# Second FFN projection of a decoder block: sixteen of 22 k tiles by seven block products, with the weight sums formed in HBM

## The chip, the cores and the metric

The kernel runs on one core of a Trainium2 chip. The metric is the device time of one execution in microseconds; times of a kernel are given as the median of its runs. All matrices are float32; TensorE takes them as fp32r.

## The reference

One decoder layer on 512 tokens of width 1024. What matters here is its second sub-layer, a SwiGLU FFN with 2816 hidden channels, and the final norm:

```python
h2 = rms_norm(x, norm2_g) * (1.0 + scale2) + shift2
f_g, f_u = jnp.split(h2 @ w_ffn_in, 2, axis=-1)          # (512, 1024) @ (1024, 5632)
x = x + gate2 * ((jax.nn.silu(f_g) * f_u) @ w_ffn_out)   # (512, 2816) @ (2816, 1024)
...
return rms_norm(x, final_norm_g)
```

Ahead of it stand the conditioning (adaLN), the combined input projection, a gated MLP mixer, a sparse attention and their projections.

## The kernel before

**Precision.** Every matrix operand is split into a rounded high part `hi` (ScalarE, a copy) and a rest `lo` (VectorE, raw minus hi). A product is three matmuls (`mm3`, L51 to L55: hi x hi, hi x lo, lo x hi). One matmul takes 128 rows of k, 128 columns of the stationary operand and up to 512 (here 256 or 512) columns of the moving one.

**Weight stream.** `add_w` enters a weight chunk of 1024 elements a partition into a list; `issue` starts its load into one of three `raw` buffers from SyncE's queue, `prep` makes `hi` and `lo` (three buffers each, L112 and L116), `ensure(upto)` does both in the list's order, and `get(i, ahead=2)` prepares two chunks beyond the one that is used.

**The order of work is written out by hand.** Each engine has one queue and runs it in the order in which the code emits. An instruction waits by semaphore for its operands and for the buffer that it overwrites; what stands behind it on its engine waits as well.

**First FFN projection.** For the steps `q` from -2 to 17 a block of 256 columns of `w_ffn_in` is multiplied as a 2 x 2 block product with seven products of blocks instead of eight (`sprod`, 256 moving columns; `s_issue` loads, `s_prep` splits the next step's weights and forms their sums). The products accumulate in PSUM tiles `R`; ScalarE copies seed one product's accumulator from another's (L1653, L1665). `gtile` holds the 22 channel tiles of silu(f_g) x f_u, `gq`. During these steps `last_mod` loads and accumulates the last section of the conditioning.

**Second FFN projection.** The 22 k tiles are in two classes. For eight (12 to 19, `KZ`) the product is again a 2 x 2 block product by seven: k halves of four tiles, token halves of 256, column halves of 512. `a_sum` forms the sums of A blocks (`gq`), `w_sub` the differences of weight blocks in SBUF, both on VectorE; `a_hi`, `a_lo`, `w_hi`, `w_lo` split; `zprod(k, ka, kw, start)` issues one product's 24 matmuls onto the accumulators `Z[k]` (PSUM tiles `pfo`, two banks each), `z_copy` seeds one accumulator from another, `z_out` and `z_add` bring one product's result to another accumulator through SBUF. The other 14 tiles (`KC`) are done directly afterwards: for both column halves `h`, chunk by chunk (two k tiles), `opt_a_mm` adds onto the same accumulators for each of four token tiles; `g_split` splits `gq`. For h = 1 the last token tile is computed in two pieces of 256 columns (`z` in the code), and the last three chunks go token tile by token tile.

**What follows a column half.** `resid` (L1162) takes a token tile of an accumulator, multiplies it by the gate (`rt`), adds the residual stream (`xr`; both VectorE) and squares it with a sum over the row (ScalarE, L1167). `scale_g` multiplies by the final gain (`xo`), `row_rstd` makes the norm's factor (GpSimd has a part), `finish` scales and stores. For h = 0 the four token tiles' `resid` and `scale_g` stand after all its chunks, beside the matmuls of h = 1.

```python
for n_, i in enumerate(ids[:-3] if h else ids):
    kts = stream[i]["kts"]
    if h == 0:
        g_split(2 * n_ + 2)
    hi, lo = get(i)
    ...
if h == 0:
    for tk in range(4):
        resid(pb[tk], 0, 512, 0, tk, gate_b[2])
        ...
        scale_g(0, 512, tk)
```

Of the kernel before, what the change touches and what calls it, by code (L numbers as in the profile page):

```python
# [9 lines left out]
F32 = mybir.dt.float32  # L10
# [18 lines left out]
def block_kernel(ctx: ExitStack, tc: tile.TileContext, x, positions, w_ada, b_ada, w_in,  # L29
# [239 lines left out]
    KZ, KC = (list(range(12, 16)), list(range(16, 20))), list(range(12)) + [20, 21]  # L269
    W_FO = [[add_w(w_ffn_out, KC[k:k + 2], 512 * h, 512) for k in range(0, len(KC), 2)] for h in range(2)]  # L270
# [1205 lines left out]
    GHOME = ["E1", None, "E3", None, "E0", None, ("S1_4", "S1_5"), ("S1_6", "S1_7"), "S2_2", "S2_3", "E7", None,  # L1476
             "S2_4", "S2_5"]
    spare = []

    def g_home(n):  # L1480
        h = GHOME[n]
        if h is None:
            return spare.pop()
        if isinstance(h, tuple):
            return [base.tile([128, S], F32R, name="gs", tag=t, bufs=1) for t in h]
        if h[0] == "S":
            t = base.tile([128, 2, S], F32R, name="gs", tag=h, bufs=1)
        else:
            t = ffn[0].tile([128, 4, S], F32R, name="gs", tag=h, bufs=1)
            spare.append((t[:, 2], t[:, 3]))  # L1490
        return t[:, 0], t[:, 1]
# [9 lines left out]
    zr, zw, za = {}, {}, {}  # L1501
    ZW = {"T1": ("E2", "E4"), "T2": ("E1", "E3"), "T3": ("E0", "E7"), "T4": ("E2", "E4"), "B22": ("E1", "E3")}
    ZA = {"A11": 0, "S1": 4, "S2": 6, "A12": 0, "S3": 4, "S4": 6, "A22": 0}

    def z_issue(name):
        kh, h = {"B11": (0, 0), "B12": (0, 1), "B21": (1, 0), "B22": (1, 1)}[name]
        for c in range(2):
            if name == "B11" or name == "B12" and c == 0:
                t = base.tile([128, 2, S], F32, name="raw", tag="raw", bufs=RAWB)
                ts = [t]  # L1510
            elif name == "B12":
                ts = [ffn[0].tile([128, 2, S], F32, name="zraw", tag="F0", bufs=1)]
            elif name == "B22":
                ts = [base.tile([128, 2, S], F32, name="zraw", tag=f"S2_{2 + c}", bufs=1)]
            else:
                ts = [base.tile([128, 1, S], F32, name="zraw", tag=f"S1_{4 + 2 * c + e}", bufs=1) for e in range(2)]
            k = KZ[kh][2 * c]
            for t in ts:
                n = t.shape[1]
                SY.dma_start(t, w_ffn_out[k * 128:(k + n) * 128, h * 512:h * 512 + 512].rearrange("(j p) n -> p j n", p=128))  # L1520
                k += n
            zr[name, c] = ts

    def z_parts(ts, *others):
        o = 0
        for t in ts:
            n = t.shape[1]
            yield (t,) + tuple(x_[:, o:o + n] for x_ in others)
            o += n

    def w_hi(key, c, src):
        if key in ZW:
            t = ffn[0].tile([128, 2, 2, S], F32R, name="zw", tag=ZW[key][c], bufs=1)
            zw[key, c] = (t[:, 0], t[:, 1])
        else:
            zw[key, c] = tuple(base.tile([128, 2, S], F32R, name=n, tag=n, bufs=3) for n in ("hi", "lo"))
        for t, hi in z_parts(zr[src, c], zw[key, c][0]):
            A.activation(hi, t, AF.Copy)

    def w_lo(key, c, src):  # L1540
        for t, hi, lo in z_parts(zr[src, c], *zw[key, c]):
            V.tensor_sub(lo, t, f(hi))

    def w_sub(o, a, b, c):

        (o_,), (b_,) = zr[o, c], zr[b, c]
        for a_, ob, bb in z_parts(zr[a, c], o_, b_):
            V.tensor_sub(ob, a_, bb)

    def a_block(name):  # L1550
        kh, th = {"A11": (0, 0), "A21": (0, 1), "A12": (1, 0), "A22": (1, 1)}[name]
        return gz[kh][:, :, th * 256:(th + 1) * 256]


    AT_ = {"A11": "A11", "A12": "A12", "A22": "A22", "S1": "A21", "S4": "A21", "S2": "A11", "S3": "A11"}

    def a_hi(key):
        za[key] = tuple(base.tile([128, 4, 256], F32R, name="za", tag=f"S2_{ZA[key] + e}", bufs=1) for e in range(2))
        A.activation(za[key][0], a_block(AT_[key]), AF.Copy)

    def a_lo(key):
        V.tensor_sub(za[key][1], a_block(AT_[key]), f(za[key][0]))

    def a_sum(key):
        a = {n: a_block(AT_[n]) for n in AT_}
        if key == "S1":
            V.tensor_add(a["S1"], a_block("A21"), a["A22"])
        elif key == "S2":
            V.tensor_sub(a["S2"], a["S1"], a["A11"])
        elif key == "S4":  # L1570
            V.tensor_sub(a["S4"], a["A12"], a["S2"])
        else:
            V.tensor_sub(a["S3"], a["A22"], a["S2"])

    def z_first():
        return [(lambda: w_hi("B11", 0, "B11"), lambda: w_lo("B11", 0, "B11")),
                (lambda: (a_hi("A11"), w_hi("B11", 1, "B11")), lambda: (a_lo("A11"), w_lo("B11", 1, "B11"))),
                (lambda: None, lambda: (w_sub("B11", "B12", "B11", 0), a_sum("S2"))),
                (lambda: (w_hi("T1", 0, "B11"), a_hi("S1")),
                 lambda: (w_sub("B11", "B12", "B11", 1), w_lo("T1", 0, "B11"), a_lo("S1")))]  # L1580
# [39 lines left out]
    for q in range(-2, NQ):  # L1620
# [8 lines left out]
        if q >= NQ - 2:  # L1629
            z_issue(("B11", "B12")[q - NQ + 2])  # L1630
# [27 lines left out]
        if q == NQ - 1:  # L1658
            z_issue("B21")
# [4 lines left out]
        sprod(R[1], S2_, TB[2], False)  # L1664
        A.activation(R[2], R[1], AF.Copy)  # L1665
# [22 lines left out]
        if q == 10:  # L1688
            for b_ in (3, 2):
                mbank[0] = b_  # L1690
                sec_tasks(one=True)
        if q == NQ - 2:
            a_sum("S1")
    z_issue("B22")
# [4 lines left out]
    def scale_g(c0, n, tk):  # L1699
        if not xo:  # L1700
            for k in range(2):
                t = ffn[0].tile([128, 2, D], F32, name="xo", tag=f"E{5 + k}", bufs=1)
                xo.extend((t[:, 0], t[:, 1]))
        cs_ = slice(c0, c0 + n)
        V.tensor_mul(xo[tk][:, cs_], xt[tk][:, cs_], fng[:, cs_])
# [10 lines left out]
    def zprod(k, ka, kw, start):  # L1716
        if start:
            Z[k] = [bank(ZB[k][e], "pfo") for e in range(2)]
        (ah, al) = za[ka]
        for c in range(2):  # L1720
            wh, wl = zw[kw, c]
            for e in range(2):
                o = slice(e * 128, (e + 1) * 128)
                for j in range(2):
                    mm3(Z[k][e], (ah[:, 2 * c + j, o], al[:, 2 * c + j, o]), (wh[:, j], wl[:, j]),
                        start and c + j == 0, c + j == 2, skip_group_check=True)

    def z_copy(dst, src):
        Z[dst] = [bank(ZB[dst][e], "pfo") for e in range(2)]
        for e in range(2):  # L1730
            A.activation(Z[dst][e], Z[src][e], AF.Copy)
# [7 lines left out]
    def z_add(dst, src):  # L1739
        for e in range(2):  # L1740
            V.tensor_add(Z[dst][e], Z[dst][e], Z["s", src][e])

    zprod(0, "A11", "B11", True)
    w_hi("T1", 1, "B11")
    a_hi("S2")
    w_lo("T1", 1, "B11")
    while left:
        left.pop(0)()
    w_sub("B11", "B22", "B11", 0)
    a_lo("S2")  # L1750
    z_copy(1, 0)
    zprod(3, "S1", "T1", True)
    w_sub("B11", "B22", "B11", 1)
    for c in range(2):
        w_hi("T2", c, "B11")
        w_lo("T2", c, "B11")
    a_hi("A12")
    w_hi("B21", 0, "B21")
    a_sum("S4")
    a_lo("A12")  # L1760
    a_sum("S3")
    z_out(3)
    zprod(1, "S2", "T2", False)
    w_hi("B21", 1, "B21")
    a_hi("S3")
    for c in range(2):
        w_lo("B21", c, "B21")
    for c in range(2):
        w_sub("B12", "B22", "B12", c)
    for c in range(2):  # L1770
        w_hi("T3", c, "B12")
    a_lo("S3")
    z_copy(2, 1)
    zprod(0, "A12", "B21", False)
    for c in range(2):
        w_lo("T3", c, "B12")
    a_hi("S4")
    for c in range(2):
        w_hi("B22", c, "B22")
    a_lo("S4")  # L1780
    for c in range(2):
        w_lo("B22", c, "B22")
    zprod(2, "S3", "T3", False)
    for c in range(2):
        w_sub("B11", "B21", "B11", c)
    a_hi("A22")
    for c in range(2):
        w_hi("T4", c, "B11")
    a_lo("A22")
    for c in range(2):  # L1790
        w_lo("T4", c, "B11")
    z_out(2)
    zprod(1, "S4", "B22", False)
    fng = ffn[0].tile([128, D], F32, name="fng", tag="F0", bufs=1)
    P.dma_start(fng, rows_bcast(final_norm_g, D))
    st["limit"] = 1 << 30
    ensure(W_FO[0][0])
    zprod(2, "A22", "T4", False)
    g_split(2)

    for h in range(2):
# [100 lines left out]
```

## Time and profile before

| | |
|---|---|
| median of 3 runs | 830.08 us (829.76 to 830.33) |
| the profiled execution | 829.8 us |
| span of its profile | 828.0 us |
| mean granted TensorE clock | 0.998 |
| PE, VectorE, ScalarE, GpSimd busy | 815.7, 672.2, 413.6, 108.5 us |
| moved by DMA | 109.10 MB, mean 132 GB/s |

The profile is one execution on the chip. PE is TensorE's matmuls, PEld its weight loads, DVE VectorE, ACT ScalarE, POOL GpSimd, SP SyncE (its queue of transfers is SPq). Times are us from the span's start, "mean ns" is of one instruction. In a timeline line stand the start, the duration, the engine, the line of the code, the operation, output and operands by the program's names, the shapes, the count, and in brackets the idle time of that engine before it with what ended it. In a windows line stand the stretch, its length, the busy time and instruction count of each engine, the granted clock, the DMA engines' busy share and GB/s. Matmuls are pipelined, so the step from one start to the next is what one costs.

### The profile page before, as it was taken

The page shows a single profiled execution, that of the slowest core. Times are in us where ns is not written, and L with a number is a line of the kernel's source. Part 1 is how long each engine was busy: PE and PEld are TensorE (multiplying, and loading weights), DVE is VectorE, ACT ScalarE, POOL GpSimd, SP SyncE. Part 2 cuts the span into 40 slices and gives each one's busy share as a digit, 9 for nine tenths or more (in the row PEclk, how much of TensorE's full clock was granted, in tenths as well). Part 3 has the DMA queues.
Part 4 walks back from the last instruction along what each step waited for, and adds up shares of the span by engine and source line. Part 5 has one row for each costly group of instructions (what it writes and reads, how often), then busy time and mean ns, then how long its engine had stood idle before and what let it go on. Part 6 is the DMA issues. An engine that isn't in the chain of part 4 may idle for free.

```text
span 828.0 us, 12858 instructions
## 1 busy us (share of the span) xinstructions
PE 815.7 (99%) x4980; PEld 730.0 (88%) x4980; DVE 672.2 (81%) x1161; ACT 413.6 (50%) x722; POOL 108.5 (13%) x101
## 2 busy tenths in 40 slices
PE   7999999999999999999999999999999999999996
PEld 6889889988888888988888899999999999888885
DVE  7989788798899558886697969799998888984635
ACT  5674544323322236665536586555555555563322
POOL 2060032362353411000000000000000000000001
PEclk9999999999999999999999999999999999999999
DMA  9974352423445562057631403445533335143212
GB/s 299 311 201 118 102 178 78 121 85 101 124 136 180 195 181 74 26 158 231 197 102 47 157 27 128 124 152 159 168 111 103 103 102 155 50 153 102 77 51 103
DMA packets 95677, 109.10 MB, mean 132 GB/s; under 512 B 5616, under 2 KB 76272, under 8 KB 95616
## 3 DMA queue, kind: packets, MB, share of 16 engines
q1 hardware_dynamic: 92512, 101.37, 40.2%
q0 software_dynamic: 2384, 6.10, 2.3%
q8 instruction: 39, 0.64, 0.3%
q10 hardware_dynamic: 720, 0.82, 0.3%
q14 instruction: 22, 0.18, 0.1%
HBM read 105.90 MB, written 2.10 MB: 130 GB/s over the span
## 4 chain that ended last, share of the span: by engine, by line
PE 96%; DMA 1%; DVE 1%; issue 0%; SPq 0%; ACT 0%; POOLq 0%; POOL 0%; DVEq 0%
PE pb L55 9%; PE pb L53 9%; PE pb L54 9%; PE R L53 8%; PE R L54 8%; PE R L55 8%; PE pfo L55 5%; PE pfo L53 5%; PE pfo L54 5%; PE pav L54 2%; PE pav L53 2%; PE pav L55 2%; PE pgb L53 2%; PE pgb L54 2%; PE pgb L55 2%; PE po L54 2%
## 5 line engine op out<-in xcount | busy, mean ns | idle before, releaser
L112 ACT ACTIVATE hi<-raw 128x1024 fp32r<-128x1024 f32 (+2 forms) x80 | 82.5, 1034 | 105.4 <-PE pb L54 39.9
L116 POOL TENSOR_TENSOR lo<-raw,hi 128x1024 fp32r<-128x1024 f32 x29 | 73.0, 2522 | 127.8 <-ACT hi L112 122.1
L116 DVE TENSOR_TENSOR lo<-raw,hi 128x1024 fp32r<-128x1024 f32 (+2 forms) x44 | 53.0, 1210 | 41.4 <-ACT hi L112 41.2
L53 PE MATMUL pb<-h,hi 128*128 128x512 f32 (+1 forms) x192 | 74.6, 388 | 0.0
L55 PE MATMUL pb<-h,lo 128*128 128x512 f32 (+1 forms) x192 | 73.9, 385 | 0.0
L54 PE MATMUL pb<-hl,hi 128*128 128x512 f32 (+1 forms) x192 | 73.9, 385 | 0.0
L177 DVE SCALAR_TENSOR_TENSOR acc<-mraw,cols,acc 128x512 f32<-128x512 f32 x49 | 40.1, 818 | 17.9 <-DMA mraw<-in_w_ada_dram 16.9
L55 PE MATMUL pfo<-hi,gs 128*128 128x512 f32 (+1 forms) x126 | 46.4, 369 | 0.0
L54 PE MATMUL pfo<-lo,gs 128*128 128x512 f32 (+1 forms) x126 | 46.4, 368 | 0.0
L53 PE MATMUL pfo<-hi,gs 128*128 128x512 f32 (+1 forms) x126 | 46.4, 368 | 0.0
L53 PE MATMUL R<-tb,sx 128*128 128x256 f32 x160 | 45.2, 282 | 0.0
L54 PE MATMUL R<-tb,sx 128*128 128x256 f32 x160 | 45.1, 282 | 0.0
L55 PE MATMUL R<-tb,sx 128*128 128x256 f32 x160 | 45.0, 281 | 0.0
L55 PE MATMUL R<-tb,lo 128*128 128x256 f32 x160 | 44.8, 280 | 0.0
L53 PE MATMUL R<-tb,hi 128*128 128x256 f32 x160 | 44.8, 280 | 0.0
L54 PE MATMUL R<-tb,hi 128*128 128x256 f32 x160 | 44.6, 279 | 0.0
L55 PEld LDWEIGHTS pb<-h,lo 128*128 128x128 f32 x192 | 36.0, 187 | 7.3
L54 PEld LDWEIGHTS pb<-hl,hi 128*128 128x128 f32 x192 | 36.0, 188 | 6.9
L53 PEld LDWEIGHTS pb<-h,hi 128*128 128x128 f32 x192 | 36.0, 188 | 6.9
L54 PE MATMUL pav<-lo,h 128*128 128x256 f32 x128 | 35.8, 279 | 0.0
L53 PE MATMUL pav<-hi,h 128*128 128x256 f32 x128 | 35.7, 279 | 0.0
L55 PE MATMUL pav<-hi,hl 128*128 128x256 f32 x128 | 35.7, 279 | 0.0
(392 smaller groups left out, 2655.4 us busy)
## 6 DMA issues: line engine op xcount, KB each, us to landing
raw<-in_w_ffn_in_dram SPq DMA_DIRECT2D x44, 512.0 KB, 4.6
raw<-in_w_in_dram SPq DMA_DIRECT2D x40, 512.0 KB, 3.9
mraw<-in_w_ada_dram SPq DMA_DIRECT2D x28, 512.0 KB, 4.1
raw<-in_w_ffn_out_dram SPq DMA_DIRECT2D x17, 512.0 KB, 3.8
s<-in_w_ada_dram SPq DMA_DIRECT2D x30, 256.0 KB, 5.6
raw<-in_w_proj_a_dram SPq DMA_DIRECT2D x8, 512.0 KB, 4.8
raw<-in_w_proj_b_dram SPq DMA_DIRECT2D x8, 512.0 KB, 4.6
raw<-in_w_in_dram SPq DMA_DIRECT2D x9, 256.0 KB, 4.7
```

The source lines that it names most:

```text
L53: T.matmul(o, wh, rh, start=start, stop=False, **kw)
L54: T.matmul(o, wh, rlo, start=False, stop=False, **kw)
L55: T.matmul(o, wlo, rh, start=False, stop=stop, **kw)
L112: A.activation(hi[:, :m], e["raw"][:, :m], AF.Copy)
L116: e["lo"].tensor_sub(lo[:, :m], e["raw"][:, :m], f(hi[:, :m]))
L177: V.scalar_tensor_tensor(o, w, cs[:, j:j + 1], o, op0=OP.mult, op1=OP.add)
```

## The change

Sixteen k tiles (4 to 19) instead of eight go by the seven products, with k halves of eight tiles; six (0 to 3, 20, 21) stay direct. A product now takes four weight chunks instead of two, 48 matmuls instead of 24. The four combinations of weight blocks that the products need are no longer formed on VectorE: GpSimd's queue issues 32 transfers of 512 KB from HBM to HBM, copies and adding transfers (`accum_op`), that build `wsum` 1 to 4; they are emitted during the steps of the first projection. All weight chunks, blocks and sums alike, now go through the common stream (`get`). A operands are in two halves (`c`), the first of which is four separate tiles of 512 columns. Signs are moved into the copies (`scale=-1.0`) and into `z_add`. The order at the end is changed: direct chunks of column half 0 come before the last product, S4 with block (1, 1), whose four chunks carry the residual steps of half 0 (`res0`); then `z_add`, then half 1's three chunks, token tile by token tile.

```diff
-    KZ, KC = (list(range(12, 16)), list(range(16, 20))), list(range(12)) + [20, 21]
-    W_FO = [[add_w(w_ffn_out, KC[k:k + 2], 512 * h, 512) for k in range(0, len(KC), 2)] for h in range(2)]
+    KZ, KC = (list(range(4, 8)) + list(range(12, 16)), list(range(8, 12)) + list(range(16, 20))), [0, 1, 2, 3, 20, 21]
+
+    dram = ctx.enter_context(tc.tile_pool(name="dram", bufs=1, space=bass.MemoryType.DRAM))
+    wsum = {n: dram.tile([1024, 512], F32, name=f"wsum{n}") for n in (1, 2, 3, 4)}
...
+    for key in ((0, 0), 1, 2, (1, 0), 3, 4):
+        add_z(key)
+    W_FO = [add_fo(0)]
+    add_z((1, 1))
+    W_FO.append(add_fo(1))
+
+    def wsum_steps():
+
+        def step(c, *moves):
+            o = slice(256 * c, 256 * c + 256)
+
+            def fn():
+                for n, add, src in moves:
+                    if isinstance(src, tuple):
+                        k = KZ[src[0]][2 * c] * 128
+                        src = w_ffn_out[k:k + 256, 512 * src[1]:512 * src[1] + 512]
+                    else:
+                        src = wsum[src][o]
+                    if add:
+                        P.dma_start(wsum[n][o], src, accum_op=OP.add)
+                    else:
+                        P.dma_start(wsum[n][o], src)
+            return fn
+
+        return [step(c, *m) for c in range(4) for m in (
+            ((1, 0, (0, 0)), (3, 0, (0, 1))), ((1, 1, (0, 1)), (3, 1, (1, 1))), ((2, 0, 1),), ((2, 1, (1, 1)),),
+            ((4, 0, 2),), ((4, 1, (1, 0)),))]
...
+    def z_first():
+        def b(k):
+            return lambda: ensure(wseq[wseq.index(W_Z[0, 0][0]) + k])
+        st["limit"] = 1 << 30
+        return [(b(0), lambda: a_hi("A11", 0), lambda: a_lo("A11", 0)),
+                (b(1), lambda: a_hi("A11", 1), lambda: a_lo("A11", 1)),
+                (lambda: None, lambda: a_sum("S2", 0)),
+                (b(2), lambda: a_sum("S2", 1))]
...
+    def zprod(k, ka, kw, start, tasks):
         if start:
             Z[k] = [bank(ZB[k][e], "pfo") for e in range(2)]
+        for c, i in enumerate(W_Z[kw]):
+            wh, wl = get(i)
+            for fn in tasks[c]:
+                fn()
+            ah, al = za[ka, c // 2]
             for e in range(2):
                 o = slice(e * 128, (e + 1) * 128)
                 for j in range(2):
+                    k_ = 2 * (c % 2) + j
+                    mm3(Z[k][e], (ah[:, k_, o], al[:, k_, o]), (wh[:, j], wl[:, j]),
+                        start and c + j == 0, c + j == 4, skip_group_check=True)
...
+    zprod(0, "A11", (0, 0), True, [[outs_left, hi_("S1", 0)], [lo_("S1", 0), hi_("S1", 1)], [lo_("S1", 1), hi_("S2", 0)],
+                                   [lo_("S2", 0), hi_("S2", 1)]])
+    z_copy(1, 0, -1.0)
+    zprod(3, "S1", 1, True, [[lo_("S2", 1)], [sm_("S4", 0), hi_("A12", 0)], [sm_("S4", 1), hi_("A12", 1)],
+                             [lo_("A12", 0)]])
     z_out(3)
+    zprod(1, "S2", 2, False, [[lo_("A12", 1)], [sm_("S3", 0)], [sm_("S3", 1), hi_("S3", 0)], [load_fng]])
+    z_copy(2, 1, -1.0)
+    zprod(0, "A12", (1, 0), False, [[lo_("S3", 0), hi_("S3", 1)], [lo_("S3", 1)], [hi_("A22", 0)],
+                                    [lo_("A22", 0), hi_("A22", 1)]])
+    zprod(2, "S3", 3, False, [[lo_("A22", 1)], [], [hi_("S4", 0)], [lo_("S4", 0), hi_("S4", 1)]])
     z_out(2)
+    zprod(2, "A22", 4, False, [[lo_("S4", 1)], [lambda: z_add(3, 2, V.tensor_sub)], [lambda: g_split(2)],
+                               [lambda: g_split(4)]])
+
+    for n_, i in enumerate(W_FO[0]):
+        hi, lo = get(i)
+        g_split(2 * n_ + 6)
         for tk in range(4):
+            opt_a_mm(Z[0][tk] if tk < 2 else Z[2][tk - 2], tk, hi, lo, stream[i]["kts"], gT, 22, False)
+    pb = [Z[0][0], Z[0][1], Z[2][0], Z[2][1]]
+
+    def res0(tk):
+        def fn():
+            resid(pb[tk], 0, 512, 0, tk, gate_b[2])
+            scale_g(0, 512, tk)
+        return fn
+
+    zprod(1, "S4", (1, 1), False, [[res0(tk)] for tk in range(4)])
+    z_add(1, 3, V.tensor_add)
+    last = bank(7, "pfo")
+    A.activation(last[:, :256], Z[3][1][:, 256:], AF.Copy)
+    pb = [Z[1][0], Z[1][1], Z[3][0], Z[3][1], last]
+    ids = W_FO[1]
+    ch = [get(i, 2 - k) for k, i in enumerate(ids)]
+    for tk in range(4):
...
```

In `zprod`, `get(i)` puts the split of the chunk after next on ScalarE's and VectorE's queues, then the `tasks` of this chunk follow, then the matmuls.

More of the change, by code (lines that the diff above doesn't have):

```diff
@@ L1483, in g_home @@
             return spare.pop()
[L1484 to L1490, printed above, removed]
+        t = ffn[0].tile([128, 4, S], F32R, name="gs", tag=h, bufs=1)
+        spare.append((t[:, 2], t[:, 3]))
         return t[:, 0], t[:, 1]
@@ L1498, in g_split @@
             gT[m] = (hi, lo)
[L1501 to L1522, printed above, removed]
@@ L1540, in w_lo @@
[L1540 to L1555, printed above, removed]
@@ L1557, in a_hi @@
[L1557 to L1573, printed above, removed]
@@ new lines, in block_kernel, with a_parts, z_sub, a_hi @@
+    AT_ = {"A11": (0, 0), "A21": (0, 1), "A12": (1, 0), "A22": (1, 1), "S1": (0, 1), "S4": (0, 1), "S2": (0, 0),
+           "S3": (0, 0)}
+    def a_parts(name, c):
+        kh, th = AT_[name]
+        o = slice(th * 256, (th + 1) * 256)
+        if c:
+            return [gz[kh][:, :, o]]
+        return [gq[4 + 4 * kh + e][:, o] for e in range(4)]
+    def z_sub(t, c):
+        return [t] if c else [t[:, e] for e in range(4)]
+    def a_hi(key, c):
+        h = ZA[key][c]
+        if isinstance(h, tuple):
+            t = tuple(base.tile([128, 4, 256], F32R, name="za", tag=n, bufs=1) for n in h)
+        else:
+            t = ffn[0].tile([128, 2, 4, 256], F32R, name="za", tag=h, bufs=1)
+            t = (t[:, 0], t[:, 1])
+        za[key, c] = t
+        for a, o in zip(a_parts(key, c), z_sub(t[0], c)):
+            A.activation(o, a, AF.Copy)
@@ L1628, in block_kernel @@
         ps = [ffn[0].tile([128, 256], F32, name="ps", tag="rt", bufs=2) for _ in range(2)]
-        if q >= NQ - 2:
-            z_issue(("B11", "B12")[q - NQ + 2])
+        if q == NQ - 2:
+            for i in W_Z[0, 0][:2]:
+                issue(i)
         t0, t1 = slice(0, 256), slice(256, 512)
@@ L1737, in z_out, with z_add @@
             A.activation(Z["s", src][e], Z[src][e], AF.Copy)
-    def z_add(dst, src):
+    def z_add(dst, src, op):
         for e in range(2):
[L1741 to L1756, printed above, removed]
```

194 lines of the change are left out of this document (71 added, 123 removed).

## The prediction

> **What bounds the kernel now.** I read the page's engine totals and slices first, then the chain that ended last.
>
> ```profile
> PE 815.7 (99%) x4980; PEld 730.0 (88%) x4980; DVE 672.2 (81%) x1161; ACT 413.6 (50%) x722; POOL 108.5 (13%) x101
> PE   7999999999999999999999999999999999999996
> DVE  7989788798899558886697969799998888984635
> PE 96%; DMA 1%; DVE 1%; issue 0%; SPq 0%; ACT 0%; POOLq 0%; POOL 0%; DVEq 0%
> ```
>
> TensorE is busy in nearly the whole span and carries 96% of the chain. So a matmul taken away counts in full, but only where nothing else then makes PE wait. The stretches that the change touches, in the windows view (PE, PEld, DVE, ACT, POOL busy us with instruction counts, granted clock, DMA share, GB/s):
>
> ```profile
> 490.00:700.00 210.00, 210.00 (x1769) 209.77 (x1769) 184.63 (x253) 123.47 (x221) 0.00 (x0) 1.00 0.42 127
> 700.00:720.00 20.00, 20.00 (x105) 16.90 (x104) 19.93 (x23) 12.62 (x17) 0.00 (x0) 1.00 0.21 71
> 720.00:740.00 20.00, 20.00 (x88) 16.14 (x87) 18.64 (x21) 12.97 (x17) 0.53 (x1) 1.00 0.32 103
> 740.00:760.00 20.00, 20.00 (x88) 16.18 (x87) 10.93 (x14) 6.56 (x10) 0.00 (x0) 1.00 0.42 135
> ```
>
> From 490 to 700 us run the first FFN projection's block products (256 columns), from 704 to 743 the seven products of the second projection (512 columns), then its direct k tiles. PE has no gap in any of them. VectorE is full in the products' 40 us (weight differences are formed there) and half idle afterwards.
>
> **Part 1: matmuls.** The tile view of the projection's accumulators, and PE's timeline over one direct chunk of 24 matmuls and the next:
>
> ```profile
> L53 PE MATMUL pfo<-hi,gs x126: 277/392/403, 743.0 to 820.6; 128*128 128x512 f32 x98, 128*128 128x256 f32 x28
> L53 PE MATMUL pfo<-zw,za x40: 389/394/400, 709.6 to 742.4; 128*128 128x512 f32 x40
> L53 PE MATMUL pfo<-hi,za x16: 392/396/400, 704.0 to 725.7; 128*128 128x512 f32 x16
> 770.78 0.39 PE L53 MATMUL pfo<-hi,gs 128*128 128x512 f32 x1
> 776.38 0.39 PE L53 MATMUL pfo<-hi,gs 128*128 128x512 f32 x1
> 781.83 0.39 PE L53 MATMUL pfo<-hi,gs 128*128 128x512 f32 x1
> ```
>
> L54 and L55 have the same counts: 3 x (98 + 40 + 16) = 462 matmuls of 512 columns and 84 of 256. A direct k tile costs 21 of 512 and 6 of 256, because the last token tile of the second column half is done in two pieces. Eight tiles fewer: 168 of 512 and 48 of 256 go. Seven products over eight k tiles instead of four add 7 x 4 x 2 x 3 = 168 of 512. What remains saved is 48 matmuls of 256 columns, at 210 us / 1769 = 0.119 us: **-5.7 us**. That is all the change can win; a matmul of 512 columns takes 0.227 to 0.233 us (5.45 and 5.60 us for 24), 0.23 below.
>
> **Part 2: the wait before the last direct tiles.** The new order ends with the three direct chunks of column half 0, then the product S4 (1,1) into the accumulators of half 1, then the addition of the saved product (`z_add`), then half 1's three chunks. Into the four chunks of that product the change puts the four residual steps of half 0. PE's next matmul accumulates onto what `z_add` writes, and `z_add` stands behind all four residuals in VectorE's queue. The same instructions, from the timeline of before:
>
> ```profile
> 776.58 1.06 ACT L112 ACTIVATE hi<-raw 128x1024 fp32r<-128x1024 f32 x1 [3.49 <-PE pfo L55]
> 777.67 1.22 DVE L116 TENSOR_TENSOR lo<-raw,hi 128x1024 fp32r<-128x1024 f32 x1 [3.17 <-ACT hi L112]
> 778.81 0.68 DVE L1165 TENSOR_TENSOR rt<-pfo,gate2b 128x512 f32<-128x512 f32 x1
> 779.53 0.69 DVE L1166 TENSOR_TENSOR xr<-xr,rt 128x512 f32<-128x512 f32 x1
> 780.26 0.63 ACT L1167 ACTIVATE rt<-xr 128x512 f32<-128x512 f32 x1 [2.62 <-DVE xr L1166]
> 780.87 0.68 DVE L1165 TENSOR_TENSOR rt<-pfo,gate2b 128x512 f32<-128x512 f32 x1
> 786.47 0.63 ACT L1167 ACTIVATE rt<-xr 128x512 f32<-128x512 f32 x1 [1.39 <-DVE xr L1166]
> 787.10 1.05 ACT L112 ACTIVATE hi<-raw 128x1024 fp32r<-128x1024 f32 x1
> ```
>
> In before the four residuals follow each other 2.06 us apart (778.81 to 780.87) under a long stretch of PE. In the changed order each is followed by the split of a further weight chunk: ScalarE can only make `hi` after the residual's Square, VectorE `lo` after `hi`, the next residual after `lo`. One round is rt to xr 0.72, to Square 0.73, to hi 0.63, to lo 1.09, to the next rt 1.14: 4.31 us, against 12 x 0.23 = 2.76 us that PE needs for a chunk. Counted from the product's first matmul (776.38 is such a moment, a chunk's first matmul): hi at 0.20, lo at 1.29, first rt at 2.43, fourth at 2.43 + 3 x 4.31 = 15.36, `z_add` at + 2.06 = 17.42, its first half done 0.69 later, at 18.1. PE ends the product at 48 x 0.23 = 11.0. **PE waits 7.1 us.** Everything behind it (three chunks, residuals, normalization) moves by that; the new tail is the old one.
>
> **Part 3: the clock after that wait.** The only long PE idle in this trace stand at its two ends:
>
> ```profile
> 4.86 9.30 PE L444 MATMUL warm<-cst 128*128 128x128 f32 x63 [4.86 <-DMA cst<-in_consts_dram]
> 6.00:8.00 2.00, 2.00 (x11) 2.00 (x10) 1.83 (x8) 1.14 (x1) 0.75 (x2) 1.00 1.02 399
> 8.00:10.00 2.00, 2.00 (x16) 2.00 (x15) 1.86 (x6) 1.20 (x4) 0.15 (x1) 1.00 1.02 394
> 10.00:12.00 2.00, 2.00 (x21) 2.00 (x20) 1.83 (x7) 1.80 (x3) 1.32 (x4) 1.00 1.15 323
> 820.83 0.28 PE L55 MATMUL pfo<-hi,gs 128*128 128x256 f32 x1
> 824.00:825.00 1.00, 0.00 (x0) 0.00 (x0) 0.09 (x1) 0.15 (x1) 0.00 (x0) 0.94 0.05 18
> 825.00:826.00 1.00, 0.00 (x0) 0.00 (x0) 0.00 (x0) 0.00 (x0) 0.00 (x0) 0.50 1.01 388
> ```
>
> PE's last matmul ends at 821.1; the granted clock is 0.94 in 824 to 825 and 0.50 after, so it fell at 824.9, 3.8 us into the idle. At the start the same matmul goes at 11 in 2 us, then 16, then 21: half pace until about 9.0, 4.2 us after PE began. A wait of 7.1 us is longer than 3.8, so PE comes back at half pace and loses half of some 4.2 us: **+2.1 us** (bounds 0, if the clock holds, and 3.5, if half pace lasts as long as the wait did). The Trainium skill, page "TensorE: Matmul & The Clock Gate", part 1 on the clock gate, has the clock halved after at least one idle window of about 3.4 us and full after a busy one; the trace's 3.8 and 4.2 agree. By its 3.4 us the loss would be an estimated 1.7 us.
>
> **Part 4: the start of the products.** In the last step of the first projection ScalarE now makes the first A operand in four pieces of 256 columns, ahead of the copy that seeds R[2]:
>
> ```profile
> 695.84 0.36 ACT L1653 ACTIVATE R<-R 128x256 f32<-128x256 f32 x1
> 696.14 0.36 ACT L1643 ACTIVATE fs<-R 128x256 f32<-128x256 f32 x1
> 697.32 1.05 ACT L1559 ACTIVATE za<-gq 128x1024 fp32r<-128x1024 f32 x1
> 699.21 0.38 ACT L1665 ACTIVATE R<-R 128x256 f32<-128x256 f32 x1
> 699.65 0.39 PE L53 MATMUL R<-tb,sx 128*128 128x256 f32 x1
> ```
>
> Before, the copy ends at 699.59 and PE needs it at 699.65. Four pieces at 0.30 put 1.2 us in; 0.54 us of idle ahead of 697.04 takes up part. **+0.6 us** (0 to 0.9).
>
> **Part 5: what is covered.** In the products VectorE loses eight weight differences and gains 14 more weight splits. Per product of 11.0 us it has four `lo`, one A operand to split and at most one A sum to form, each of these two as large as two `lo`: 8 x 1.14 = 9.1 us. A raw buffer is taken for 3.8 us of landing, 1.1 of hi and 1.1 of lo, 6.0 us; three of them must turn round in 8.3. Without that cover each late us is a us. The formation of sums, 32 moves of 512 KB, stands on GpSimd's queue:
>
> ```profile
> DMA  9974352423445562057631403445533335143212
> q1 hardware_dynamic: 92512, 101.37, 40.2%
> raw<-in_w_ffn_out_dram SPq DMA_DIRECT2D x17, 512.0 KB, 3.8
> 486.27 0.57 POOL L1404 DMA_DIRECT2D gate2b<-in_b_ada_dram  x1
> 727.62 0.53 POOL L1795 DMA_DIRECT2D fng<-in_final_norm_g_dram  x1 [240.78 <-DVE zw L1542]
> ```
>
> Nothing else is on that queue from 486 to 727, so the moves start about 487, each after the one it depends on; nobody waits behind them except the final gain's load, used 60 us later. Price: 101.37 MB took 0.402 x 828 = 333 us of all 16 engines, so 512 KB takes 1.72. No row shows a transfer that adds; its bounds are one load's price (32 moves, 55 us) and, with four times that for the 16 adds, 138 us. I take twice (reads two operands): 83 us. With 0.42 x 210 = 88 us of present use in the 210 us, 171 fit. Cost 0, with the rival below as its other end.
>
> **Sum.** -5.7 + 7.1 + 2.1 + 0.6 = +4.1 us. The profiled execution took 829.8 us (span 828.0 and 1.8 around it), 0.3 under the median: 833.9 for it, **834.2 us** for the median.
>
> **Rivals.** *The clock holds* (it falls later into an idle here, or the wait is under 3.8): +2.0, 832.1 us; the two ends of the trace speak against it. *The adds are dear*: at 3 times a load's price the engines are full (88 + 28 + 16 x 1.72 x 3 = 199), and loads and sums come late. At four times 226 us are wanted of 210, 16 us more: 850 us. For it: no row bounds an add, and the DMA slices show 0.4 to 0.5 from 520 to 600 against 0.3 in the 80 us after; against: sums are needed only from about 705, loads are issued a step ahead. *Faster*: the wait is 3r - 5.8 us for a round of r us; without Part 3 the change gains if r is under 3.5. If ScalarE and VectorE had the chunks' splits done ahead, r would be 2.06 and the wait 0.4: 830.1 - 5.7 + 0.6 + 0.4 = 825.4 us. Against: only three hi/lo buffers, and both queues run in the order written, in which the 2.62 and 1.39 us of ScalarE's waits on xr stand.
>
> **How the numbers follow.** Forecast 0.60, clock holds 0.17, dear adds 0.15, faster 0.06, and 0.02 for a wait so short that the terms cancel. A measurement of this kernel can tell about 0.2%, 1.7 us. Faster by more: 0.06. Within: 0.08 (0.02 and some third of the clock case, whose 2.0 us lies close). Slower: 0.86. Range: the clock case with Part 4 at 0 and the wait 0.5 shorter gives 831.0; above, Part 3's 3.5 and a first part of the dear adds give 840.0.
>
> **What would show it.** Right: one PE gap near 7 us ahead of the last 90 matmuls, put down to `z_add`; the granted clock at 0.5 after it; 498 matmuls on these accumulators; a gap under 1 us before the R[2] products. Wrong: no such gap, or gaps of PE between 490 and 700 with DMA share near 1, or waits for sums after 710.

## The result, and the profile after

| | before | after |
|---|---|---|
| median | 830.21 us (829.76 to 830.75) | 837.23 us (835.77 to 837.75) |
| ratio, 95% interval | | 1.0081 [1.0064, 1.0099] |
| the profiled execution, its span | 829.8, 828.0 us | 837.66, 835.9 us |
| mean granted clock | 0.998 | 0.992 |

The change makes the kernel 7.0 us slower; the forecast was 834.2 us in a range of 831.0 to 840.0. The page of after: engine totals, the slices of PE and VectorE, the chain that ended last.

```profile
PE 813.8 (97%) x4932; PEld 726.4 (87%) x4932; DVE 681.2 (81%) x1191; ACT 423.7 (51%) x746; POOL 131.2 (16%) x133
PE   7999999999999999999999999999999999999965
DVE  7989788798899558886797878899999888877465
PE 57%; DVE 14%; DMA 4%; ACT 2%; issue 1%; POOLq 0%; POOL 0%; ACTq 0%; DVEq 0%
```

PE is less busy than before, 813.8 us against 815.7, in a longer span; the last two slices of PE read 6 and 5, where before had 9 and 6. The chain now runs through VectorE, 14% against 1%. The waits view (engine, tile and line that waited, what it waited for: total us, times, longest) names both places, and the chain's pieces (start, us) show what the long one is made of:

```profile
PE pfo L53 <- DVE pfo L1758: 7.1, 1, 7.1
PE R L53 <- ACT R L1675: 0.4, 1, 0.4
```

```profile
794.20 0.96 ACT hi L112
795.18 1.22 DVE lo L116
796.41 0.61 DVE rt L1210
797.05 0.70 DVE xr L1211
797.90 0.47 issue
798.55 0.96 ACT hi L112
...
805.11 0.61 DVE rt L1210
805.75 0.70 DVE xr L1211
...
807.08 0.70 DVE pfo L1758
807.92 0.77 PE pfo L53
808.69 0.43 PE pfo L54
...
812.10 0.41 PE pfo L53
812.51 0.23 PE pfo L54
```

```profile
797.83 0.63 ACT L1212 ACTIVATE rt<-xr 128x512 f32<-128x512 f32 x1 [2.68 <-DVE xr L1211]
```

One round: `hi` on ScalarE, `lo` on VectorE, the residual's `rt` and `xr`, then 0.47 us that the chain calls issue and that the timeline, in the second fence, fills with the Square on ScalarE, then the next `hi`. 794.20 to 798.55 is 4.35 us. After the fourth comes `z_add` (L1758), and only then PE's first matmul of the last tiles, 7.1 us late. Those matmuls start 0.43 us apart until 812.5, 0.23 after. In the windows view the clock of that place, and the stretch of the first projection beside the moves:

```profile
490.00:700.00 210.00, 210.00 (x1769) 209.73 (x1768) 186.69 (x260) 124.03 (x225) 22.51 (x31) 1.00 0.75 205
805.00:810.00 5.00, 2.08 (x5) 1.72 (x6) 4.53 (x7) 1.97 (x4) 0.00 (x0) 0.55 0.00 0
810.00:815.00 5.00, 5.00 (x18) 3.92 (x18) 0.59 (x1) 0.00 (x0) 0.00 (x0) 0.76 0.00 0
```

The clock's deficit there, 0.45 and 0.24 of 5 us, is 3.45 us, so 6.9 us at half. In 490 to 700 the DMA share went from 0.42 to 0.75 with PE full. The tile view of the accumulators, and from the page GpSimd's transfers (packets, MB, share of 16 engines' span) and the issues (KB, us to landing):

```profile
L53 PE MATMUL pfo<-hi,za x112: 389/395/500, 705.9 to 800.0; 128*128 128x512 f32 x112
L53 PE MATMUL pfo<-hi,gs x54: 277/395/767, 772.8 to 826.5; 128*128 128x512 f32 x42, 128*128 128x256 f32 x12
```

```profile
q0 software_dynamic: 8144, 22.88, 11.4%
wsum<-in_w_ffn_out_dram POOLq DMA_DIRECT2D x24, 512.0 KB, 8.4
```

Before, q0 was

```profile
q0 software_dynamic: 2384, 6.10, 2.3%
```

11.4% of 835.9 less 2.3% of 828.0 us: the 32 moves took 76 us of all 16 engines, 2.4 each.

**Where 7.9 us of the profiled executions are** (829.8 to 837.66; first and last matmul of each stage in the two traces): the stages ahead of the change ended 1.2 us later, which no other kernel with this change repeated; the first projection took 0.7 us more, 0.4 of it the wait on R; the second took 120.8 us from first to last matmul against 116.8, so +4.0; from there to the end 1.9 more. The last 1.9 us are in no part of the prediction. The last store lands at 826.5 before and 832.4 after, and the span ends 1.5 and 3.5 us later. What stands there in the trace, though none of the views lists it, is GpSimd's closing instruction, DRAIN:

| kernel | transfers that GpSimd issues | DRAIN starts | lasts | span ends |
|---|---|---|---|---|
| before | 36 | 822.81 | 3.73 us | 828.0 |
| after | 68 | 828.73 | 6.34 us | 835.9 |

### The profile page after: what moved, and what is told of

The parts are those of the page before. It is cut to its first block, busy times and chain, and to the rows that moved or that the text cites. A ratio compares the mean times of both kernels' runs of the same rounds, so it can differ in the third digit from the quotient of the medians.

```text
span 835.9 us, 12907 instructions
## 1 busy us (share of the span) xinstructions
PE 813.8 (97%) x4932; PEld 726.4 (87%) x4932; DVE 681.2 (81%) x1191; ACT 423.7 (51%) x746; POOL 131.2 (16%) x133
## 3 DMA queue, kind: packets, MB, share of 16 engines
q0 software_dynamic: 8144, 22.88, 11.4%
## 4 chain that ended last, share of the span: by engine, by line
PE 57%; DVE 14%; DMA 4%; ACT 2%; issue 1%; POOLq 0%; POOL 0%; ACTq 0%; DVEq 0%
PE R L53 8%; PE R L54 8%; PE R L55 8%; DMA mraw<-in_w_ada_dram 4%; PE pfo L53 4%; PE pfo L55 4%; PE pfo L54 4%; DVE acc L177 3%; DVE sco L704 2%; DVE m L700 2%; PE pb L53 2%; PE pb L55 2%; PE pb L54 2%; PE po L54 2%; PE po L53 2%; PE po L55 2%
## 5 line engine op out<-in xcount | busy, mean ns | idle before, releaser
L112 ACT ACTIVATE hi<-raw 128x1024 fp32r<-128x1024 f32 (+2 forms) x100 | 103.8, 1039 | 101.3 <-PE pb L54 44.4
L116 DVE TENSOR_TENSOR lo<-raw,hi 128x1024 fp32r<-128x1024 f32 (+2 forms) x64 | 77.6, 1216 | 37.1 <-ACT hi L112 36.8
L53 PE MATMUL pfo<-hi,za 128*128 128x512 f32 x112 | 44.2, 395 | 0.0
L55 PE MATMUL pfo<-hi,za 128*128 128x512 f32 x112 | 44.1, 394 | 0.0
L54 PE MATMUL pfo<-lo,za 128*128 128x512 f32 x112 | 44.1, 394 | 0.0
L1216 POOL TENSOR_TENSOR sm<-sm,mhalf 128x1 f32<-128x1 f32 x8 | 5.3, 659 | 237.6 <-DVE sm L1215 237.6
```

What stands on the lines that cost most here:

```text
L53: T.matmul(o, wh, rh, start=start, stop=False, **kw)
L54: T.matmul(o, wh, rlo, start=False, stop=False, **kw)
L55: T.matmul(o, wlo, rh, start=False, stop=stop, **kw)
L112: A.activation(hi[:, :m], e["raw"][:, :m], AF.Copy)
L116: e["lo"].tensor_sub(lo[:, :m], e["raw"][:, :m], f(hi[:, :m]))
L1216: P.tensor_tensor(r2[:, tk:tk + 1], r2[:, tk:tk + 1], mhalf[:, :1], op=OP.pow)
```

## The experiments

My theory after the result: the wait of 7.1 us, the half clock behind it and the wait on R are what the prediction said, and the moves, costed at nothing, cost 2 us or more, most of it in the DRAIN. The rivals: the moves do not matter and the rest is the new order; or it is the DMA load in the first projection.

**1. The moves alone.** Before, with the 32 moves emitted at the same places and their result unused.

```diff
         sprod(R[1], S2_, TB[2], False)
+        if wsteps:
+            wsteps.pop(0)()
```

> The kernel before with the 32 transfers that form the sums added at the same places of the first projection; nothing reads the sums. The changed kernel's profile is 7.9 us longer than that of before, of which 1.2 us stand ahead of the first projection and 1.9 us after the last store. Theory 1 (the transfers cost nothing on the path, those 3.1 us are the difference between two executions): 830.2 us, within 0.5. Rival (the transfers or the HBM tiles cost at the program's start and end, or delay the first projection): 832 to 834 us, with the 1.9 us after the last store again.

Measured: 831.92 us against 829.79, ratio 1.0035 [1.0022, 1.0047]: +2.1. The profile has a DRAIN of 6.34 us. It also has two waits in the first projection that before does not have; but it is of an execution of 833.49 us, one of the two longest of five, and the other three took 831.68 to 831.92:

```profile
PE R L53 <- ACT R L1680: 0.8, 1, 0.8
PE R L53 <- ACT ps L1701: 0.4, 1, 0.4
```

**2. The change without the moves.** The products read plain weight blocks, so the sums of weights are left out of the result; the order is the changed one.

```diff
-                src, k0, c0 = wsum[key], 2 * c, 0
+                src, k0, c0 = w_ffn_out, KZ[key % 2][2 * c], 512 * (key // 3)
-    wsteps = wsum_steps()
+    wsteps = []
```

> The changed kernel without the 32 transfers: the products that used sums read plain weight blocks instead, as many loads of the same size (the result is not the reference's). Theory 1: PE waits 7.1 us for the addition as in the changed kernel and the time stays within 1 us of its 837. Rival (the transfers cost): 833.5 to 835, the 3.1 us outside the products gone, with the 7.1 us wait unchanged.

Measured: 834.29 us, ratio 1.0054 [1.0042, 1.0067]: +4.5, next to the forecast's sum of +4.1. The DRAIN lasts 3.73 us again. PE's long wait is unchanged:

```profile
PE pfo L53 <- DVE pfo L1758: 7.1, 1, 7.1
PE R L53 <- ACT R L1675: 0.4, 1, 0.4
```

So of the 7.0 us, 4.5 are the matmuls and the order, and 2.5 come with the moves.

**3. The wait filled.** 26 matmuls that nobody uses, into a free bank, stand ahead of the last direct tiles. They keep PE busy and change nothing else.

```diff
+    fill = bank(4, "fill")
+    for _ in range(26):
+        T.matmul(fill, gT[0][0][:, :128], gT[0][0], start=True, stop=True)
     pb = [Z[1][0], Z[1][1], Z[3][0], Z[3][1], last]
```

> The changed kernel with 26 matmuls of 512 columns, of no use, put on PE between the product S4 and the last direct chunks, onto a free accumulator: 26 x 0.23 = 6.0 us of the 7.1 us wait filled. Theory (the wait costs 7.1 us and the clock's fall 2.1 more): the granted clock stays at 1, the ten matmuls at half pace go, 2.1 us less than the changed kernel, 835.1 us; the end of the wait does not move. Rival (the clock's fall costs nothing, since VectorE or ScalarE set the pace behind it): no difference.

Measured: 835.12 us, ratio 1.0063 [1.0049, 1.0076], 2.1 us under after; from first to last matmul the second projection takes 118.8 us, 2.0 less than after. The wait and the windows of the same stretch:

```profile
PE pfo L53 <- DVE pfo L1758: 1.2, 1, 1.2
```

```profile
805.00:810.00 5.00, 3.83 (x17) 2.90 (x16) 4.77 (x7) 1.97 (x4) 0.00 (x0) 1.00 0.00 0
810.00:815.00 5.00, 5.00 (x23) 4.02 (x22) 2.31 (x4) 0.00 (x1) 0.00 (x0) 1.00 0.00 0
```

26 x 0.23 + 1.2 = 7.2 us: the data come no sooner, only the clock stays up. The clock's drop is worth 2.0 to 2.1 us.

**4. The addition first.** `z_add` moves from behind the four residuals to the first direct chunk of half 0.

```diff
-    z_add(1, 3, V.tensor_add)
...
         g_split(2 * n_ + 6)
+        if n_ == 0:
+            z_add(1, 3, V.tensor_add)
```

> The changed kernel with the addition of the saved product moved ahead, to the first direct chunk of column half 0; the residual steps stay in the product S4. Theory (the residuals' rounds of 4.3 us are the cause, the addition only the place where PE meets them): PE now waits for the splits of the last two weight chunks instead, some 6 us in several pieces of 1 to 2.3 us, none of them long enough for the clock to fall: 3 us less than the changed kernel, 834.2 us. Rival (the addition in PSUM itself is the cause): no wait is left, 9 us less, 828 us.

Measured: 838.02 us, ratio 1.0095 [1.0081, 1.0108]: no gain, against the expectation. The waits, PE's timeline lines that stand behind one, and the windows:

```profile
PE pfo L53 <- ACT hi L112: 2.4, 2, 1.6
PE pfo L54 <- DVE lo L116: 1.2, 2, 0.8
```

```profile
802.76 0.50 PE L53 MATMUL pfo<-hi,gs 128*128 128x512 f32 x1 [1.56 <-ACT hi L112]
804.02 0.80 PE L54 MATMUL pfo<-lo,gs 128*128 128x512 f32 x1 [0.76 <-DVE lo L116]
...
805.89 0.63 PE L55 MATMUL pfo<-hi,gs 128*128 128x512 f32 x1
807.40 0.80 PE L53 MATMUL pfo<-hi,gs 128*128 128x512 f32 x1 [0.88 <-ACT hi L112]
808.66 0.80 PE L54 MATMUL pfo<-lo,gs 128*128 128x512 f32 x1 [0.46 <-DVE lo L116]
```

```profile
800.00:805.00 5.00, 2.68 (x9) 1.65 (x8) 3.89 (x6) 1.67 (x3) 0.00 (x0) 0.90 0.00 0
805.00:810.00 5.00, 3.65 (x8) 2.10 (x7) 2.21 (x3) 1.97 (x4) 0.00 (x0) 0.50 0.00 0
810.00:815.00 5.00, 5.00 (x14) 3.89 (x14) 2.79 (x5) 1.34 (x3) 0.56 (x1) 0.57 0.00 0
```

The wait halves, to 3.6 us, but in four pieces, each behind the `hi` or `lo` of the next chunk, since the splits still stand behind the residuals. The clock falls all the same (the next matmul starts are 0.43 apart), although the longest piece is 1.56 us: from 801 to 804 only one matmul was begun. And it stays down longer: the deficit 0.10, 0.50, 0.43 of 5 us is 10.3 us at half, which costs 5.1 us where the one long wait cost 3.45 of granted time, part of it while PE had nothing to do. By the Trainium skill, page "TensorE: Matmul & The Clock Gate", part 1, the clock is set by how busy PE was in free-running windows of about 3.4 us; two and three of them, an estimated 6.8 and 10.2 us, agree with the 6.9 and 10.3 measured. It is not the length of one gap that counts here but how little PE does in such a stretch: in the 3.41 us ahead of the fall (800.63 to 804.04) PE was busy for 1.09 us, and in kernel 2 a stretch as long with 1.70 us of work (797.65 to 801.07) left the clock at 1.00.

The profile is of the shortest of the four executions (835.92 us; the others took 837.67 to 838.44). There the second projection takes 120.1 us against 120.8 in after, so the wait that was halved brought 0.7 us where 3 were expected: 111.5 us, what 5 below takes without these waits and with the clock up, and 3.6 of waits and 5.1 of half clock make 120.2. What the three longer executions have beside it no profile shows.

**5. The residuals out of the way.** As 4, and each Square stands one chunk behind its residual, the fourth residual behind the last chunks' splits.

```diff
-    zprod(1, "S4", (1, 1), False, [[res0(tk)] for tk in range(4)])
+    zprod(1, "S4", (1, 1), False, [[res0(0)], [sq0(0), res0(1)], [sq0(1), res0(2)], [sq0(2)]])
...
     ch = [get(i, 2 - k) for k, i in enumerate(ids)]
+    res0(3)()
+    sq0(3)()
```

> The changed kernel with the four residuals of column half 0 taken out of the way of the last weight splits: z_add stands in the first direct chunk, each Square one chunk behind its residual, and the fourth residual behind the last chunks' splits. My theory (the wait is made by the order on ScalarE and VectorE, the round of 4.31 us): no PE wait over 1 us at the end of the products, the clock stays at 1.00, first to last matmul of the second projection near 111.5 us (before 116.8, less 5.7, plus small change); what is left against before is -5.7, +2.0 at the end of the program and +0.4 to +1.7 of waits in the first projection: 826.5 to 828.0 us. Rival (VectorE has too much work in the products whatever the order, and the wait comes back in pieces as with the early addition): waits of 2 to 4 us, a clock below 0.995, 832 us or more.

Measured: 827.31 us against 829.9, ratio 0.9973 [0.9964, 0.9983]: 10 us under after by the order of a dozen instructions, and now faster than before. The second projection takes 111.5 us from first to last matmul (704.5 to 815.9). All of PE's waits that the view lists:

```profile
PE warm L489 <- DMA cst<-in_consts_dram: 4.6, 1, 4.6
PE R L53 <- ACT R L1675: 0.4, 1, 0.4
```

The first is the wait for the program's first load, which before has too.

**6. The first operand behind the copy.** As 5, with `a_hi("A11", 0)` after the copy that seeds R[2].

```diff
-        return [(b(0), lambda: a_hi("A11", 0), lambda: a_lo("A11", 0)),
+        return [(b(0),),
                 (b(1), lambda: a_hi("A11", 1), lambda: a_lo("A11", 1)),
-                (lambda: None, lambda: a_sum("S2", 0)),
+                (lambda: a_hi("A11", 0), lambda: (a_lo("A11", 0), a_sum("S2", 0))),
```

> As the kernel with the residuals apart, and ScalarE makes the first A operand of the second projection behind the copy that seeds R[2], not ahead of it. My theory (Part 4's wait comes from that order): PE's wait for ScalarE on R goes from 0.4 to 0, and the time is 0.4 to 0.9 us below the kernel with the residuals apart: 826.0 to 827.3 us. Rival (the operand is now late for the projection's first product): a new wait of 0.5 to 1 us ahead of the first matmul of the second projection, no gain.

Measured: 827.53 us, ratio 0.9969 [0.9959, 0.9979]: not told apart from 5. The wait at 699 us (L1675 in 5) is gone, but the profiled execution, 828.13 us, has others at 612 and 618, amid the moves:

```profile
PE R L53 <- ACT R L1661: 0.8, 1, 0.8
PE R L53 <- ACT ps L1682: 0.7, 1, 0.7
```

What stands ahead of these waits is another load than that of the weights. VectorE's timeline in the same trace:

```profile
607.14 1.54 DVE L177 SCALAR_TENSOR_TENSOR acc<-mraw,cols,acc 128x512 f32<-128x512 f32 x2 [2.35 <-DMA mraw<-in_w_ada_dram]
```

VectorE waited 2.35 us for `mraw`, the load of the conditioning's last section (`last_mod`), and the next step's weight sums stood behind it in its queue; ScalarE waited 2.90 us for these sums, and the copies that PE needs stood behind its splits. The eight times fall into 826.4 to 827.0 and 828.1 to 828.3; the waits' 1.5 us would account for the difference, but only one of the eight has a profile.

**7. The same without the moves.** As 6, with the edit of 2; again the sums of weights are left out of the result.

> As the kernel with residuals apart and the operand behind the copy, without the 32 moves: the products read plain weight blocks in place of the sums, so the sums of weights are left out of the result. It is the price of the moves when nothing else is wrong. My theory: -5.7 and nothing else, 824.0 to 824.6 us; with the 32 small moves' kernel beside it, the moves cost 2.0 to 3.0 us, nearly all of it at the program's end. Rival (the moves' cost was hidden behind the wait and the order, and is under 1 us): the two agree within 1 us.

Measured: 824.99 us, ratio 0.9940 [0.9926, 0.9953]; no wait of PE on R or on the accumulators, a DRAIN of 3.73 us. The moves cost 6 some 2.5 us, as they cost the changed kernel.

**8. Fewer, bigger moves.** As 6, with 8 moves of 2 MB for 32 of 512 KB.

```diff
-            o = slice(256 * c, 256 * c + 256)
+                    dst = wsum[n].rearrange("(g r) n -> r g n", g=2)
...
-        return [step(c, *m) for c in range(4) for m in (
+        return [step(0, *m) for m in (
```

> As the kernel before it in this list, but the sums are formed by 8 moves of 2 MB in place of 32 of 512 KB: the same bytes with 44 transfers issued by GpSimd where there were 68. My theory (what the moves cost at the end is GpSimd's closing DRAIN, which grows with the number of transfers, 3.73 us for 36 and 6.34 for 68, so about 4.4 for 44): the end of the program comes 1.5 to 1.9 us after the last store's landing in place of 3.5, and the time is 824.5 to 825.6 us. Rival (the DRAIN goes by the bytes or descriptors, which are the same): 3.5 us at the end, and the time of the kernel before it. Second rival (bigger moves hold loads up in the first projection): R waits above 1.7 us, 826 or more.

Measured: 841.75 us, ratio 1.0145 [1.0131, 1.0158]. The first theory was right on the DRAIN and wrong on the time. The DRAIN lasts 4.38 us for 44 transfers, and the end comes 1.5 us after the last store. The bytes are the same as in 6 and the queue's packets more (8656 against 8144), so of the three it is the number of transfers that the DRAIN follows. But the loads were held up, as the second rival said, and the kernel is 14 us slower than 6. Waits, two windows with the clock, the moves' issue line:

```profile
PE R L53 <- ACT R L1674: 10.4, 3, 5.6
PE R L53 <- ACT R L1660: 2.3, 2, 1.5
PE R L53 <- ACT ps L1681: 1.7, 1, 1.7
```

```profile
500.00:520.00 20.00, 18.48 (x154) 18.07 (x153) 14.08 (x20) 10.84 (x22) 4.70 (x2) 1.00 1.06 260
520.00:540.00 20.00, 13.36 (x100) 12.96 (x98) 8.56 (x12) 5.11 (x8) 1.30 (x1) 0.91 1.08 269
```

```profile
wsum<-in_w_ffn_out_dram POOLq DMA_DIRECT2D x6, 2048.0 KB, 21.1
```

While a move of 2 MB is under way (21.1 us to landing, against 8.4 for 512 KB) the DMA engines are full (share 1.06 and 1.08), the first projection's weights come late (VectorE waits 18.4 us for them between 500 and 560), PE has 13.4 us of work in 20, and the clock drops there too.

**9. Nothing on GpSimd at the end.** As 6, with the last four row factors made by a root on ScalarE and a reciprocal on VectorE.

```diff
-        P.tensor_tensor(r2[:, tk:tk + 1], r2[:, tk:tk + 1], mhalf[:, :1], op=OP.pow)
+            A.activation(r2[:, tk:tk + 1], r2[:, tk:tk + 1], AF.Sqrt)
+            V.reciprocal(r2[:, tk:tk + 1], r2[:, tk:tk + 1])
```

> As the kernel with residuals apart and the operand behind the copy (827.53 us), but the last four row factors (the inverse roots that GpSimd makes at L1216, the last one at 817.96 in the profile with the residuals apart) are made by a root on ScalarE and a reciprocal on VectorE, so that GpSimd has nothing left to do after the load of the final gain near 725 us. My theory: the closing DRAIN of 6.34 us starts when GpSimd's last instruction is done; it now runs long before the end and costs nothing: end of program 1.3 to 1.5 us after the last store, 2.0 us less, 825.0 to 826.0 us. Rival (the DRAIN stands behind a meeting of all engines): it still starts at the end and the time stays within 0.5 us of 827.5.

Measured: 824.87 us (824.47 to 824.95), ratio 0.9936 [0.9923, 0.9950]: faster than before by 5.3 us and than after by 12. The DRAIN now runs from 694.5 to 701.1, in the middle of the program, and the span ends 1.5 us after the last store. With all 32 moves the time is that of 7, which has none. From the last matmul's start to the end it is 7.1 us where 6 has 9.1; the rest of the 3.6 us between the two spans stands mostly in the first projection, where this trace has none of 6's waits.

**10. The moves spread.** As 9, with the moves given out in groups of five and three (four on average) behind every second section of the first projection.

```diff
+        if not u:
+            if q >= 0:
+                P.tensor_copy(pace, gtile(2 * g - 2)[:, :1])
+            for _ in range(3):
+                if wsteps:
+                    wsteps.pop(0)()
```

> As the kernel just before it in this list, and the 32 moves are given out four at a time, one group behind each second section of the first projection (a one-column copy on GpSimd of a tile that the section has written holds the group back), so that they reach to about 690 us where they ended at 635. My theory (the 0.4 to 1.7 us of PE waits on R come from stretches in which loads and moves fill the DMA engines, a share of 0.8 to 1.06 from 500 to 640): the share stays under 0.95 in windows of 20 us, R waits go under 0.5 us, 0.3 to 1.2 us less than without the pacing. Rival (the waits come from bursts within a group, which pacing does not thin out): R waits of 0.4 us or more, no difference over 0.3 us. Second rival: the last sums come late, waits on weights at the start of the second projection.

Measured: 826.33 us, ratio 0.9956 [0.9944, 0.9969], 1.5 us slower than 9. The moves ended about 660, the DMA share stayed at 0.91 or less in all windows of 20 us, and waits on R were there:

```profile
PE R L53 <- ACT R L1666: 1.6, 2, 0.8
PE R L53 <- ACT ps L1685: 0.3, 1, 0.3
```

Kernel 9 had shares up to 1.05 in the same windows and no such wait. So the share over 20 us does not tell when a load comes late; my theory of these waits fell, and the rival (bursts) is only argued: its "no difference" does not fit either. Here too VectorE had waited for `mraw` ahead of them, 2.0 us at 567 and 1.6 at 608; in 9 it waited 0.3 us once.

**11. The control.** Before, with the edit of 9 alone.

> The kernel before with the last four row factors made on ScalarE and VectorE, nothing else: the control for the two others. Theory: before, the closing DRAIN ended with the last store's landing and the end came 1.5 us later, so there is nothing to win there; the factor itself takes about as long as on GpSimd: within 0.7 us of 829.9. Rival: the hop to GpSimd and back is itself worth 0.5 to 1.5 us at the end, or the root costs a table load on ScalarE there (0.5 to 1.5 us more).

Measured: 830.01 us against 830.16, ratio 0.9997 [0.9989, 1.0006]. The factors' new place is worth nothing by itself; the 2.0 us that 9 won at the program's end, it won from the DRAIN behind the moves.

| kernel | transfers that GpSimd issues | DRAIN starts | lasts | last store lands | span ends |
|---|---|---|---|---|---|
| 1, moves alone | 68 | 824.54 | 6.34 us | 828.2 | 831.7 |
| 8, big moves | 44 | 836.76 | 4.38 us | 840.4 | 841.9 |
| 9, nothing on GpSimd at the end | 68 | 694.54 | 6.61 us | 821.2 | 822.7 |
| 10, moves spread | 68 | 696.21 | 7.80 us | 823.1 | 824.5 |
| 11, control | 36 | 728.38 | 6.53 us | 827.2 | 828.8 |

## Why the prediction was right, and where it was not

**Part 1** holds: 3 x (112 + 54) = 498 matmuls, and with waits and clock out of the way the second projection took 111.5 us in 5, 7 and 9 against 116.8: -5.3 of the -5.7.

**Part 2** holds to the tenth: a wait of 7.1 us, put down to `z_add`, from rounds of 4.30 to 4.35 us where 4.31 were worked out. Experiment 5 shows that the order made it: with the same work in another order it is gone.

**Part 3** holds: 2.1 forecast, 2.0 to 2.1 won back by the filling. The bound of 3.5, "if half pace lasts as long as the wait did", came close to what was granted low (3.45) by coincidence; part of that fell into the wait itself.

**Part 4** holds: a wait of 0.4 us, but R's matmuls took 200.8 us from first to last in after, 2 and 5 against 200.2 in 7 and 9, where the operand stands behind the copy, so 0.6 as forecast. Experiment 6 took the wait away by its cause.

These four sum to +4.1; without the moves the kernel measured +4.5, and the four as measured (-5.3, 7.1, 2.1, 0.6) make it.

**Part 5** is the step that failed, in the part that said "nobody waits behind them" and "Cost 0". The price of a move was about right (76 us of 16 engines, 83 estimated), the splits were covered, the sums were there in time. But the moves cost 2.5 us: 2.0 at the end of the program, where GpSimd's DRAIN had grown from 3.73 to 6.34 us and now ended after the last store (1.5 us between store and end became 3.5), and the rest, in some executions, in waits of 1.2 to 1.9 us in the first projection. In before the DRAIN was hidden, with little to spare: it ended at 826.53, as the store landed at 826.5. Where it ends last (after, 1, 3 to 6) the span ends 0.8 us behind it; where the store does, 1.4 to 1.6 us behind the store. So it could have grown by some 0.7 us unseen, and grew by 2.6. I asked who waits behind the moves on GpSimd's queue and looked only at the program's own instructions.

**The range.** That the time lies in it owes something to luck: its upper end stood for a longer half pace and for dear adds, neither of which came, and it left room for a cost at the end of the program that no part named.

**The rivals.** *The clock holds* is out by the windows, *the adds are dear* by the share of 0.75 with PE full from 490 to 700; but 8 shows how near that cliff is. *Faster* was given 825.4 us if the splits were not behind the residuals; in the kernel as written they were, and the kernels that put them apart reached 827.3, and 824.9 with the DRAIN hidden. (Its limit for a round, "under 3.5", should be 3.6 by its own terms: 3r - 5.8 has to stay under 5.7 - 0.6.)

## What to carry to other kernels

Walk the new order of a hand-written schedule in rounds: where one task of engine A, then B, then A again stands between two chunks, the round and not the busy share sets the pace, and moving a dozen instructions was worth 10 us here, more than the matmuls that the change saved. Ask of work moved to an idle engine what it leaves to do at the end of the program, not only who waits for its results. Before breaking one long wait into pieces, look whether TensorE does enough between them: with four waits of 3.6 us together the second projection took 120.1 us, with one of 7.1 it took 120.8.

## What the hardware did that was not expected

GpSimd's closing DRAIN grows with the transfers that the engine has issued: at the end of the program 3.73, 4.38 and 6.34 us for 36, 44 and 68, which is 0.08 us for each more. Placed earlier, right behind the issue of the final gain's load, it does not go by that: 6.53 us for 36 in 11, 6.61 and 7.80 for 68 in 9 and 10. There it ended 1.8, 3.1 and 3.1 us after the last packet of that load, so a wait for the load fits all three, but it was not tried. A DRAIN of 6.6 us in mid-program cost nothing.

TensorE's clock fell in a stretch whose longest idle piece was 1.56 us, and stayed at half for 10.3 us while further short waits followed. Within each trace, the changes of the granted clock lie whole multiples of 3.413 us apart (805.53, 812.36 and 829.42 in after; 804.04 and 814.28 in 4). Cut at these marks, all thirteen traces agree: at full clock, every stretch of 3.41 us with 0 to 1.1 us of PE work was followed by half clock (after: 0 and 1.03; 4: 1.09; 8: 0.63), and none with 1.68 us or more (8: 1.68; 2: 1.70; after: 2.10). Where the limit lies between the two, no run shows.

The first projection waited 1.2 to 1.9 us beside the moves in the traces of 1, 3, 6 and 10, and, but for Part 4's wait, not at all in those of after, 4, 5 and 9, with much the same DMA load. In the first four VectorE had waited 2.0 to 2.4 us at one time for `mraw`; in the others, and in the kernels without moves, never longer than 0.5 us. In 6 that load took 12.4 us to land between 590 and 620 us, in after 7.6, in before 6.7. So, as these timelines read, one late load of the conditioning holds up what stands behind it in VectorE's queue. Why it is late in one execution and not in another stays open, and no run gave it another place.
